# Gates of two chunks from one fp32r product with stacked halves, in a hybrid decoder layer

## The chip, the cores and the metric

The kernel runs on one core of one Trainium2 chip, as one launch. The metric is the device time of that launch in microseconds; the median of three runs is shown, and one further execution was taken with the hardware profiler. The engines are named as in the profile: PE is the matrix engine (PEld its weight loads), DVE the vector engine, ACT the scalar engine, POOL the general engine, SP the engine that issues the DMAs.

## The reference, cut to what matters

One layer of a decoder over 2048 tokens and 16 meta tokens, width 1024, in fp32: an input projection, then side by side a gated linear attention (GLA, 4 heads) and a sliding-window attention, an output projection, and a feed-forward block of width 4096. The change is in the gates of the GLA part:

```
g = log_sigmoid(lr @ w_gate_up + b_gate) / 16     # lr: (tokens, 16), w_gate_up: (16, 256)
b = cumsum(g) within a chunk
o = (A v) + (q * exp(b)) S                        # A from q, k and exp of differences of b
S = exp(b_last) * S + (k * exp(b_last - b))^T v
```

## The kernel before

The dense products (input projection, output projection, feed-forward) split each fp32 operand into a high and a low part of type fp32r and run three fp32r matmuls of 512 columns (lines 160 to 162) for each fp32 one. They are the bulk of PE's work. The two attention parts are Python generators, `gla` and `swa`; the dense code calls `mix_stage` after every 12 matmuls of a product, and each generator then emits its next stage. So the small matmuls of the attention parts stand between the dense ones. The final order of the first half of the program (until about 1100 us) is set by a scheduler that works with its own estimates of durations; engines run their instructions in that order. From there on the order is written out by hand and is not touched.

GLA goes through a chunk of 16 meta tokens and then 16 chunks of 128 tokens, called chunk 0 to chunk 15 here. Each chunk starts with `gates`: a PE transpose of lr (tile `lr`, line 567), a DVE copy into `lrT` (line 568), two plain fp32 matmuls of 128 columns into `z` (line 572; the profile records each as two), three ACT steps and one DVE step of the log-sigmoid into `g` (lines 543 to 546), and two DVE scans into `B` (line 580). `lrT` holds ones below its 16 rows, so that row 16 of the weight `wg` adds the bias. After that come seven levels (`E`, `kl`, `ql` on DVE and ACT, the matmul `lv`, line 677, and the predicated copy `AT`, line 682), `qB` (line 721), the output matmuls `o` and the state update. `sg` is the log-sigmoid of another gate at the end of a chunk, 512 columns wide, with the same four lines 543 to 546.

The projection's weights come in with `raw` and are split by ACT (`wh`, line 125) and DVE (`wl`, line 126). The rotary part of the projection's results is a run of DVE steps (lines 203 to 206) behind the copy `st` (line 243) that empties a PSUM bank.

Of the kernel before, what the change touches and what calls it, by code (L numbers as in the profile page):

```python
# [35 lines left out]
class Layer:  # L36
# [23 lines left out]
    def more_consts(self):  # L60
        nc, a, cp = self.nc, self.a, self.cp
        t = cp.tile([P, 576], F32, name="tabs", tag="tabs")
        nc.sync.dma_start(out=t, in_=a["tabs"])
        self.ident, self.smask = t[:, 0:P], t[:, P:544]
        self.csm = t[:, 544:576].rearrange("p (a n) -> p a n", a=2)
        wide = self.np_.tile([P, len(LEVELS), 64], U32, name="lwide", tag="sq", bufs=3)
        nc.sync.dma_start(out=wide, in_=a["lmask"])
        self.lmask = cp.tile([P, len(LEVELS), 64], U8, name="lmask", tag="lmask")
        nc.vector.tensor_copy(self.lmask, wide)
        self.wg = cp.tile([P, 256], F32, name="wg", tag="wg")  # L70
        nc.sync.dma_start(out=self.wg, in_=a["wg"])
        self.nsink = cp.tile([P, 8], F32, name="nsink", tag="nsink")
        nc.vector.tensor_scalar(self.nsink, self.sinks, -1.0, None, ALU.mult)
# [474 lines left out]
    def gla_setup(self, cp):  # L548
# [6 lines left out]
        for t in self.kl:  # L555
            nc.gpsimd.memset(t, 0.0)
        self.lrT = cp.tile([P, P], F32, name="lrT", tag="lrT")
        nc.vector.memset(self.lrT, 1.0)
# [24 lines left out]
    def decayed_keys(self, gp, B, k, n):  # L583

        nc = self.nc
        kt = gp.tile([P, 2, P], F32, name="kt", tag="g", bufs=1)[:, :, :n]
        nc.vector.tensor_tensor(kt, B[:, :, n - 1 : n].to_broadcast([P, 2, n]), B, ALU.subtract)
# [24 lines left out]
    def gla_load(self, b, gp):  # L612
        nc = self.nc
        qk = gp.tile([P, 4, P], F32, name="qk", tag="qk", bufs=2)
        nc.sync.dma_start(out=qk, in_=self.feat[b // 4, :, F_Q:F_R, (b % 4) * P : (b % 4 + 1) * P])
        v = gp.tile([P, 528], F32, name="v", tag="v", bufs=2)
        nc.sync.dma_start(out=v, in_=self.vals[b, :, 0:528])
        return qk, v

    def gla(self, gp):  # L620
        nc = self.nc
        while self.have_v < 1:
            yield
        ld = self.gla_load(0, gp)
        B = yield from self.gates(gp, self.m_v[:, 512:528], NM)
        kt = self.decayed_keys(gp, B, self.m_k, NM)
# [10 lines left out]
        for b in range(nblk):  # L637
            qk, v = ld
            if b + 1 < nblk:
                while self.have_v <= b + 1:  # L640
                    yield
                ld = self.gla_load(b + 1, gp)
            yield from self.gla_chunk(b, gp, qk, v)
            self.done_g = b + 1
# [41 lines left out]

    def gla_chunk(self, b, gp, qk, v):
# [3 lines left out]
        B = yield from self.gates(gp, v[:, 512:528], P)  # L691
        nc.gpsimd.tensor_copy(self.qpad[0:64, 0], q[0:64])
# [16 lines left out]
        for li in range(len(LEVELS)):  # L709
# [37 lines left out]
        for hp in range(2):  # L747
            for h in range(2):
                rr = slice(64 * h, 64 * h + 64)
                c = hp * 256 + h * P  # L750
                nc.vector.scalar_tensor_tensor(
                    self.S[rr, hp, h, :], self.S[rr, hp, h, :], eB[rr, hp, P - 1 : P], ps[rr, c : c + P],
                    ALU.mult, ALU.add,
                )
# [883 lines left out]
def layout(inp):  # L1638
# [15 lines left out]
    A["w2q"] = f["w_ff2"][0].reshape(16, 2, P, 4, 2, P).transpose(0, 2, 4, 1, 3, 5).reshape(16, P, 2048)  # L1654
    A["wg"] = np.concatenate([f["w_gate_up"][0], f["b_gate"], np.zeros((P - 17, 256), np.float32)], axis=0)
    pos = np.arange(L) + NM
# [37 lines left out]
```

## Time and profile before

| | |
|---|---|
| median of 3 runs (lowest to highest) | 2172.25 us (2171.24 to 2172.98) |
| profiled execution | 2170.22 us, span of the trace 2168.5 us |
| PE busy | 99% of the span |
| DVE, ACT, POOL busy | 71%, 48%, 9% |
| mean granted PE clock | 0.997 |

The span is what the trace covers; the 1.7 us around it belong to the launch. A busy share of PE counts modelled ends of pipelined matmuls: matmuls follow each other closer than their durations, so start times, not durations, tell what one costs.

### The profile page before, as it was taken

Reading aid. Unit: us, or ns where it says so; the run is one execution under the profiler, and the core shown is the slowest. Engines: PE = TensorE matmul, PEld = TensorE weight load, DVE = VectorE, ACT = ScalarE, POOL = GpSimd, SP = SyncE. Lnnn points to the kernel's source line nnn. Section 1 sums busy time; section 2 is a strip of 40 time slices with the busy share of each in tenths; the row PEclk is TensorE's granted clock in tenths of the full one; section 3 lists DMA queues with packets and bytes.
Section 4 is the critical chain, followed back from the end, with each engine's and each line's share of the span. In section 5 each row is a group of like instructions: output and inputs, shape, how many; then the busy total and the mean of one; then the engine's idle time right before and its main releaser. Section 6 shows DMA issues by size and latency. Waiting matters only on the chain.

```text
span 2168.5 us, 29105 instructions
## 1 busy us (share of the span) xinstructions
PE 2141.0 (99%) x10423; PEld 1801.7 (83%) x10423; DVE 1537.9 (71%) x2863; ACT 1046.4 (48%) x2156; POOL 198.8 (9%) x311
## 2 busy tenths in 40 slices
PE   8999999999999999999999999999999999999997
PEld 6998789788888888888888888888888888888886
DVE  7167884988987878789963445456867766685866
ACT  5132754456665656566652323353544545333434
POOL 2000111121221122221110000000000000000001
PEclk9999999999999999999999999999999999999998
DMA  6234533335333333335333335544355557754412
GB/s 212 95 96 134 157 108 111 99 103 188 106 105 104 100 110 105 104 109 168 112 101 99 97 97 155 184 142 141 121 162 178 170 194 264 279 173 138 156 39 78
DMA packets 147857, 292.51 MB, mean 135 GB/s; under 512 B 12288, under 2 KB 64000, under 8 KB 147712
## 3 DMA queue, kind: packets, MB, share of 16 engines
q1 hardware_dynamic: 147712, 290.66, 42.0%
q8 instruction: 82, 1.34, 0.3%
q14 instruction: 63, 0.52, 0.1%
HBM read 220.68 MB, written 69.86 MB: 134 GB/s over the span
## 4 chain that ended last, share of the span: by engine, by line
PE 87%; DVE 7%; ACT 3%; DMA 1%; issue 1%; DVEq 0%; SPq 0%; ACTq 0%
PE psd L162 16%; PE psd L161 16%; PE psd L160 16%; PE psq L160 4%; PE psq L162 4%; PE psq L161 4%; PE psw L160 4%; PE psw L161 4%; PE psw L162 4%; PE lv L677 2%; PE psd L295 2%; PE psd L296 2%; PE psd L297 2%; PE pv L530 1%; DVE wl L126 1%
## 5 line engine op out<-in xcount | busy, mean ns | idle before, releaser
L125 ACT ACTIVATE wh<-raw 128x1024 fp32r<-128x1024 f32 (+2 forms) x190 | 199.1, 1048 | 343.7 <-PE psd L162 297.2
L126 DVE TENSOR_TENSOR wl<-raw,wh 128x1024 fp32r<-128x1024 f32 (+2 forms) x190 | 234.0, 1232 | 74.5 <-ACT wh L125 73.9
L160 PE MATMUL psd<-f,wh 128*128 128x512 f32 x512 | 203.2, 397 | 0.0
L160 PE MATMUL psd<-hid,wh 128*128 128x512 f32 x512 | 202.9, 396 | 0.0
L162 PE MATMUL psd<-f,wh 128*128 128x512 f32 x512 | 200.0, 391 | 0.0
L161 PE MATMUL psd<-f,wl 128*128 128x512 f32 x512 | 199.9, 390 | 0.0
L162 PE MATMUL psd<-hid,wh 128*128 128x512 f32 x512 | 199.7, 390 | 0.0
L161 PE MATMUL psd<-hid,wl 128*128 128x512 f32 x512 | 199.7, 390 | 0.0
L160 PE MATMUL psd<-u,wh 128*128 128x512 f32 x416 | 167.7, 403 | 3.7 <-DVE st L241 2.4
L161 PE MATMUL psd<-u,wl 128*128 128x512 f32 x416 | 163.9, 394 | 3.1 <-DVE wl L126 3.0
L162 PE MATMUL psd<-u,wh 128*128 128x512 f32 x416 | 164.5, 396 | 0.6 <-DVE u L156 0.6
L160 PE MATMUL psw<-bh,wh 128*128 128x512 f32 x392 | 152.5, 389 | 0.0
L161 PE MATMUL psw<-bh,wl 128*128 128x512 f32 x392 | 152.5, 389 | 0.0
L162 PE MATMUL psw<-bl,wh 128*128 128x512 f32 x392 | 152.5, 389 | 0.0
L160 PE MATMUL psq<-oh,wh 128*128 128x512 f32 x384 | 149.8, 390 | 0.0
L162 PE MATMUL psq<-ol,wh 128*128 128x512 f32 x384 | 149.4, 389 | 0.0
L161 PE MATMUL psq<-oh,wl 128*128 128x512 f32 x384 | 149.4, 389 | 0.0
L962 ACT ACTIVATE wh<-rw 128x1024 fp32r<-128x1024 f32 x49 | 52.0, 1061 | 149.7 <-PE psw L162 132.9
L162 PEld LDWEIGHTS psd<-f,wh 128*128 128x128 f32 x512 | 96.1, 188 | 20.8 <-DVE f L156 0.2
L162 PEld LDWEIGHTS psd<-hid,wh 128*128 128x128 f32 x512 | 96.1, 188 | 20.5
L160 PEld LDWEIGHTS psd<-hid,wh 128*128 128x128 f32 x512 | 96.2, 188 | 19.3 <-issue 0.2
L161 PEld LDWEIGHTS psd<-hid,wl 128*128 128x128 f32 x512 | 96.2, 188 | 19.1 <-issue 0.2
(315 smaller groups left out, 5163.3 us busy)
## 6 DMA issues: line engine op xcount, KB each, us to landing
raw<-w SPq DMA_DIRECT2D x132, 512.0 KB, 3.7
b<-hops SPq DMA_DIRECT2D x49, 512.0 KB, 3.5
raw<-wo SPq DMA_DIRECT2D x32, 512.0 KB, 3.8
r<-w SPq DMA_DIRECT2D x32, 512.0 KB, 4.2
rw<-w2q SPq DMA_DIRECT2D x28, 512.0 KB, 6.6
raw<-wf SPq DMA_DIRECT2D x26, 512.0 KB, 4.0
feat<-st SPq DMA_DIRECT2D x52, 256.0 KB, 2.2
hops<-t SPq DMA_DIRECT2D x42, 256.0 KB, 5.0
```

Source lines behind the costliest of these rows:

```text
L125: nc.scalar.activation(wh, raw, AF.Copy)
L126: nc.vector.tensor_tensor(wl, raw, wh.bitcast(F32), ALU.subtract)
L160: nc.tensor.matmul(ps, lhsT=wh, rhs=ah, start=first, stop=False, skip_group_check=skip)
L161: nc.tensor.matmul(ps, lhsT=wl, rhs=ah, start=False, stop=False, skip_group_check=skip)
L162: nc.tensor.matmul(ps, lhsT=wh, rhs=al, start=False, stop=last, skip_group_check=skip)
L295: nc.tensor.matmul(ps, lhsT=ah, rhs=wh, start=kt == 0, stop=False)
L296: nc.tensor.matmul(ps, lhsT=ah, rhs=wl, start=False, stop=False)
L297: nc.tensor.matmul(ps, lhsT=al, rhs=wh, start=False, stop=kt == KT - 1)
L530: nc.tensor.matmul(pv, lhsT=v[:, kv, :], rhs=t, start=i == 0 and t is ph, stop=False)
L677: nc.tensor.matmul(ps[:, hp * P : (hp + 1) * P], lhsT=kl[:, hp, :], rhs=ql[:, :, hp, :], start=True, stop=True)
L962: nc.scalar.activation(wh, src, AF.Copy)
```

## The change

One call of `gates` now serves two chunks (the meta chunk still goes alone). The two transposes of lr go into one PSUM tile of 256 columns. `lrT` becomes an fp32r tile of 256 columns in which rows 0 to 15 and 64 to 79 hold the high part of lr and rows 32 to 47 the low part; the weight `wgr` holds high, high and low parts in the same rows. So one fp32r matmul for each half of the 256 outputs gives all three partial products. The scans of both chunks follow, and the second chunk of a pair starts without gates. lr gets a DMA of its own for each pair; the weight's DMA moves from `more_consts` into `gla`; `g` and `kt` move into the buffers of `sg` and `qB`; the exponential of `B` goes straight into `qB`, and only its last column is kept as `eB`.

```diff
-        self.wg = cp.tile([P, 256], F32, name="wg", tag="wg")
-        nc.sync.dma_start(out=self.wg, in_=a["wg"])
...
-    def gates(self, gp, lr, n):
+    def gates(self, gp, lrs, n):
         nc = self.nc
+        m = len(lrs)
+        w = m * n
         ps = self.gpsum("lr")
-        nc.tensor.transpose(ps[:16, :n], lr, self.ident[:n, :n])
-        nc.vector.tensor_copy(self.lrT[0:16, :n], ps[:16, :n])
+        for j, lr in enumerate(lrs):
+            nc.tensor.transpose(ps[:16, j * n : (j + 1) * n], lr, self.ident[:n, :n])
+        rows = self.lrT.rearrange("p a n -> p (a n)")
+        nc.scalar.activation(rows[0:16, :w], ps[:16, :w], AF.Copy)
+        nc.vector.tensor_tensor(rows[32:48, :w], ps[:16, :w], rows[0:16, :w].bitcast(F32), ALU.subtract)
+        nc.scalar.activation(rows[64:80, :w], ps[:16, :w], AF.Copy)
         yield
         ps = self.gpsum("z")
         for hp in range(2):
             nc.tensor.matmul(
-                ps[:, hp * n : (hp + 1) * n], lhsT=self.wg[:, hp * P : (hp + 1) * P], rhs=self.lrT[:, :n],
+                ps[:, hp * w : (hp + 1) * w], lhsT=self.wgr[:, hp * P : (hp + 1) * P], rhs=rows[:, :w],
                 start=True, stop=True,
             )
-        B = gp.tile([P, 2 * P], F32, name="B", tag="B")[:, : 2 * n]
-        g = gp.tile([P, 2 * P], F32, name="g", tag="g", bufs=1)[:, : 2 * n]
-        self.log_sigmoid(ps[:, : 2 * n], g)
-        for c in (slice(0, n), slice(n, 2 * n)):
-            nc.vector.tensor_tensor_scan(B[:, c], self.ones[:, :n], g[:, c], 0.0, ALU.mult, ALU.add)
-        return B.rearrange("p (a n) -> p a n", a=2)
+        B = gp.tile([P, m, 2, n], F32, name="B", tag="B" if m > 1 else "E", bufs=1 if m > 1 else 2)
+        g = gp.tile([P, NB], F32, name="g", tag="sg", bufs=1)[:, : 2 * w]
+        self.log_sigmoid(ps[:, : 2 * w], g)
+        for j in range(m):
+            for hp in range(2):
+                c = slice(hp * w + j * n, hp * w + (j + 1) * n)
+                nc.vector.tensor_tensor_scan(B[:, j, hp, :], self.ones[:, :n], g[:, c], 0.0, ALU.mult, ALU.add)
+            if j == 0 and m > 1:
+                yield
+        return [B[:, j] for j in range(m)]
...
+        if b % 2 == 0:
+            self.lr = gp.tile([P, 2, 16], F32, name="lr", tag="lr", bufs=2)
+            nc.sync.dma_start(out=self.lr, in_=self.vals[b : b + 2, :, 512:528].rearrange("b p c -> p b c"))
...
+        wg = gp.tile([P, 256], F32, name="wg", tag="qB", bufs=1)
+        wh = gp.tile([P, 256], F32R, name="wgh", tag="kT", bufs=1)
+        nc.sync.dma_start(out=wg, in_=self.a["wg"])
+        nc.scalar.activation(wh, wg, AF.Copy)
+        nc.scalar.activation(self.wgr[0:64], wg[0:64], AF.Copy)
+        nc.vector.tensor_tensor(self.wgr[64:P], wg[64:P], wh[64:P].bitcast(F32), ALU.subtract)
...
+            if b % 2 == 0:
+                Bs = yield from self.gates(gp, [self.lr[:, j, :] for j in range(2)], P)
...
-        eB = gp.tile([P, 2, P], F32, name="eB", tag="eB", bufs=1)
-        nc.scalar.activation(eB, B, AF.Exp, scale=1.0 / 16.0)
+        eB = gp.tile([P, 2, 1], F32, name="eB", tag="eB")
+        nc.scalar.activation(eB, B[:, :, P - 1 : P], AF.Exp, scale=1.0 / 16.0)
         qB = gp.tile([P, 2, P], F32, name="qB", tag="qB", bufs=1)
-        nc.vector.tensor_tensor(qB, q, eB, ALU.mult)
+        nc.scalar.activation(qB, B, AF.Exp, scale=1.0 / 16.0)
+        nc.vector.tensor_tensor(qB, q, qB, ALU.mult)
```

The scheduler makes a new order of the first half from this. Line numbers of the changed kernel differ by 2 above the change and by some 20 below it. Three places follow, each as it was and as it is.

PE at the start of chunk 8, where the product `z` stands between dense matmuls. Before:

```order
L160 MATMUL psd<-hid,wh 128x512
L161 MATMUL psd<-hid,wl 128x512
L162 MATMUL psd<-hid,wh 128x512
L572 MATMUL z<-lrT,wg 128x128 x2
L160 MATMUL psd<-hid,wh 128x512
L161 MATMUL psd<-hid,wl 128x512
```

And with the change:

```order
L158 MATMUL psd<-hid,wh 128x512
L159 MATMUL psd<-hid,wl 128x512
L160 MATMUL psd<-hid,wh 128x512
L578 MATMUL z<-lrT,wgr 128x256 x2
L158 MATMUL psd<-hid,wh 128x512
L159 MATMUL psd<-hid,wl 128x512
```

The place is the same, the two matmuls are twice as wide and of the other type, and at the start of chunk 9 there are none.

DVE late in the second half of the input projection, around the split `wl` of one certain weight (the 33rd one on this engine in both programs) and amid the steps of chunk 3. Before:

```order
L205 TENSOR_TENSOR st<-st,cs 128x512
L503 TENSOR_TENSOR pm_117<-trm,pm_117 64x128
L206 TENSOR_TENSOR st<-st,sw 128x512
L514 TENSOR_TENSOR pl<-tr,ph 128x512
L682 COPY_PREDICATED AT<-lmask,lv 128x256
L721 TENSOR_TENSOR qB<-qk,eB 128x256
L126 TENSOR_TENSOR wl<-raw,wh 128x1024
L695 TENSOR_TENSOR qkp<-qk 128x256
L243 TENSOR_TENSOR st<-psd,rb 128x512
```

And with the change, around the same weight:

```order
L703 COPY_PREDICATED AT<-lmask,lv 128x32x8
L680 TENSOR_TENSOR E<-B 128x256 x2
L414 TENSOR_TENSOR qs<-ft,qs 64x512
L684 TENSOR_TENSOR kl_123<-qk,E 128x64x2
L688 TENSOR_TENSOR ql<-qpad,E 128x256
L124 TENSOR_TENSOR wl<-raw,wh 128x1024
L241 TENSOR_TENSOR st<-psd,rb 128x512
L703 COPY_PREDICATED AT<-lmask,lv 128x64x4
L201 STREAM_SHUFFLE sw<-st 128x512
L684 TENSOR_TENSOR kl_122<-qk,E 128x128
```

Before, the split stood behind all seven levels of chunk 3 and behind `qB`; now it stands behind the fourth level's copy, so three levels and `qB` come after it, and two rotary runs (16 of them stood ahead before, 14 do now).

SP at the start of the program (`x` is the input, `wf` weights of the projection, `cs` rotary tables, `xm` the meta tokens). Before:

```order
L215 DMA x<-x 128x1024
L71 DMA wg<-wg 128x256
L122 DMA raw<-wf 128x1024
L182 DMA xm<-meta 128x128
L215 DMA x<-x 128x1024
L326 DMA cs<-cs 128x1024
```

And with the change:

```order
L213 DMA x<-x 128x1024
L180 DMA xm<-meta 128x128
L120 DMA raw<-wf 128x1024
L324 DMA cs<-cs 128x1024
L213 DMA x<-x 128x1024 x3
```

The gate weight's transfer has left this place (it now stands later, between two of the last transfers of `x`), and the table `cs` has moved ahead of the third transfer of `x`.

## Rows read from the trace of the kernel before

**Rows 1.** The page: busy time of the engines, and the last chain's shares.

```profile
PE 2141.0 (99%) x10423; PEld 1801.7 (83%) x10423; DVE 1537.9 (71%) x2863; ACT 1046.4 (48%) x2156; POOL 198.8 (9%) x311
PE 87%; DVE 7%; ACT 3%; DMA 1%; issue 1%; DVEq 0%; SPq 0%; ACTq 0%
```

**Rows 2.** PE's timeline around the last `z`: start us, us, what.

```profile
1029.38 0.61 PE L572 MATMUL z<-lrT,wg 128*128 128x128 f32 x4
1029.75 0.48 PE L160 MATMUL psd<-m,wh 128*128 128x512 f32 x1
1030.06 0.40 PE L161 MATMUL psd<-m,wl 128*128 128x512 f32 x1
1030.29 0.39 PE L162 MATMUL psd<-m,wh 128*128 128x512 f32 x1
```

**Rows 3.** PE's timeline near the end: fp32r matmuls of 256 columns.

```profile
2149.92 0.28 PE L162 MATMUL psd<-l,h 128*128 128x256 f32 x1
2150.04 0.28 PE L160 MATMUL psd<-h 128*128 128x256 f32 x1
```

**Rows 4.** Tile `z`: durations in ns, min/median/max.

```profile
L543 ACT ACTIVATE g<-z x17: 197/365/386, 113.3 to 1030.2; 128x256 f32<-128x256 f32 x16, 128x32 f32<-128x32 f32 x1
L546 DVE SCALAR_TENSOR_TENSOR g<-z,g x17: 192/424/426, 114.1 to 1031.9; 128x256 f32<-128x256 f32 x16, 128x32 f32<-128x32 f32 x1
```

**Rows 5.** Groups by line and shape: scans, and the 512-column log-sigmoid `sg`.

```profile
L580 DVE TENSOR_TENSOR_SCAN B<-ones,g 128x128 f32<-128x128 f32 x32 | 12.9, 445 | 0.2
L546 DVE SCALAR_TENSOR_TENSOR sg<-r,sg 128x512 f32<-128x512 f32 x16 | 11.3, 709 | 10.4 <-ACT sg L545 10.3
L543 ACT ACTIVATE sg<-r 128x512 f32<-128x512 f32 x16 | 10.1, 629 | 12.8 <-DVE mo L770 11.8 <-DMA r<-feat 0.9
```

**Rows 6.** Tile `lr`: the copy into `lrT`.

```profile
L568 DVE COPY lrT<-lr x17: 163/269/279, 107.4 to 1027.0; 16x128 f32<-16x128 f32 x16, 16x16 f32<-16x16 f32 x1
```

**Rows 7.** The chain that ended last, from 374 to 425 us.

```profile
420.68 1.58 DVE wl L126
422.30 0.50 PE psd L161
```

**Rows 8.** PE's timeline behind that wait (idle before it in brackets).

```profile
422.30 0.50 PE L161 MATMUL psd<-u,wl 128*128 128x512 f32 x1 [1.95 <-DVE wl L126]
423.41 0.63 PE L162 MATMUL psd<-u,wh 128*128 128x512 f32 x1
425.97 0.63 PE L162 MATMUL psd<-u,wh 128*128 128x512 f32 x1
```

**Rows 9.** Windows: busy us (instructions) of each engine, granted clock, DMA.

```profile
core 0: us, PE busy (x) PEld busy (x) DVE busy (x) ACT busy (x) POOL busy (x), PEclk, DMA share, GB/s
410.00:420.00 10.00, 10.00 (x52) 8.11 (x51) 9.79 (x20) 3.71 (x11) 1.14 (x3) 1.00 0.21 68
420.00:430.00 10.00, 8.05 (x37) 6.53 (x36) 8.25 (x14) 1.96 (x11) 1.17 (x2) 0.83 0.70 215
```

**Rows 10.** PE's timeline at the first level of chunk 1.

```profile
269.87 0.68 PE L677 MATMUL lv<-ql,kl 128*128 128x128 f32 x4 [0.72 <-DVE ql L667]
```

**Rows 11.** The chain that ended last, from 240 to 271 us.

```profile
264.94 0.34 DVE g L546
265.87 1.30 DVE B L580 x2
```

**Rows 12.** PE's timeline at the one `z` that waited.

```profile
708.36 0.71 PE L572 MATMUL z<-lrT,wg 128*128 128x128 f32 x4 [0.28 <-DVE lrT L568]
```

**Rows 13.** PE's timeline from 32 us, behind its longest early wait.

```profile
32.07 0.47 PE L160 MATMUL psd<-u,wh 128*128 128x512 f32 x1 [2.21 <-DVE st L241]
32.38 0.39 PE L161 MATMUL psd<-u,wl 128*128 128x512 f32 x1
32.61 0.39 PE L162 MATMUL psd<-u,wh 128*128 128x512 f32 x1
```

**Rows 14.** SP's timeline at the start: DMA issues.

```profile
8.04 0.43 SPq L71 DMA_DIRECT2D wg<-wg  x1
11.51 0.33 SPq L215 DMA_DIRECT2D x<-x  x1
11.88 0.43 SPq L326 DMA_DIRECT2D cs<-cs  x1
```

**Rows 15.** The chain that ended last, at the start: transfers it waits for.

```profile
1.71 4.82 DMA x<-x
11.51 5.34 DMA x<-x
```

More of the change, by code (lines that the diff above doesn't have):

```diff
@@ L556, in gla_setup @@
             nc.gpsimd.memset(t, 0.0)
-        self.lrT = cp.tile([P, P], F32, name="lrT", tag="lrT")
-        nc.vector.memset(self.lrT, 1.0)
+        self.lrT = cp.tile([P, 2, P], F32R, name="lrT", tag="lrT")
+        nc.vector.tensor_scalar(self.lrT, self.ones.unsqueeze(1).to_broadcast([P, 2, P]), 1.0, None, ALU.mult)
+        self.wgr = cp.tile([P, 256], F32R, name="wgr", tag="wgr")
     def gpsum(self, name):
         return self.pm.tile([P, NB], F32, name=name, tag="gl", bufs=2)
-    def gates(self, gp, lr, n):
+    def gates(self, gp, lrs, n):
         nc = self.nc
+        m = len(lrs)
+        w = m * n
         ps = self.gpsum("lr")
-        nc.tensor.transpose(ps[:16, :n], lr, self.ident[:n, :n])
-        nc.vector.tensor_copy(self.lrT[0:16, :n], ps[:16, :n])
+        for j, lr in enumerate(lrs):
[4 more added lines that the diff above has]
+        nc.scalar.activation(rows[64:80, :w], ps[:16, :w], AF.Copy)
         yield
@@ L572, in gates @@
             nc.tensor.matmul(
[L573 removed]
+                ps[:, hp * w : (hp + 1) * w], lhsT=self.wgr[:, hp * P : (hp + 1) * P], rhs=rows[:, :w],
                 start=True, stop=True,
             )
[L576 to L581 removed]
+        B = gp.tile([P, m, 2, n], F32, name="B", tag="B" if m > 1 else "E", bufs=1 if m > 1 else 2)
[8 more added lines that the diff above has]
+        return [B[:, j] for j in range(m)]
     def decayed_keys(self, gp, B, k, n):
         nc = self.nc
[L586 removed]
+        kt = gp.tile([P, 2, P], F32, name="kt", tag="qB", bufs=1)[:, :, :n]
         nc.vector.tensor_tensor(kt, B[:, :, n - 1 : n].to_broadcast([P, 2, n]), B, ALU.subtract)
@@ L613, in gla_load @@
         nc = self.nc
+        if b % 2 == 0:
+            self.lr = gp.tile([P, 2, 16], F32, name="lr", tag="lr", bufs=2)
+            nc.sync.dma_start(out=self.lr, in_=self.vals[b : b + 2, :, 512:528].rearrange("b p c -> p b c"))
         qk = gp.tile([P, 4, P], F32, name="qk", tag="qk", bufs=2)
         nc.sync.dma_start(out=qk, in_=self.feat[b // 4, :, F_Q:F_R, (b % 4) * P : (b % 4 + 1) * P])
-        v = gp.tile([P, 528], F32, name="v", tag="v", bufs=2)
-        nc.sync.dma_start(out=v, in_=self.vals[b, :, 0:528])
+        v = gp.tile([P, NB], F32, name="v", tag="v", bufs=2)
+        nc.sync.dma_start(out=v, in_=self.vals[b, :, 0:NB])
         return qk, v
@@ L621, in gla @@
         nc = self.nc
-        while self.have_v < 1:
+        while self.have_v < 2:
             yield
+        wg = gp.tile([P, 256], F32, name="wg", tag="qB", bufs=1)
[4 more added lines that the diff above has]
+        nc.vector.tensor_tensor(self.wgr[64:P], wg[64:P], wh[64:P].bitcast(F32), ALU.subtract)
         ld = self.gla_load(0, gp)
-        B = yield from self.gates(gp, self.m_v[:, 512:528], NM)
+        (B,) = yield from self.gates(gp, [self.m_v[:, 512:528]], NM)
         kt = self.decayed_keys(gp, B, self.m_k, NM)
@@ L638, in gla @@
             qk, v = ld
+            if b % 2 == 0:
+                Bs = yield from self.gates(gp, [self.lr[:, j, :] for j in range(2)], P)
             if b + 1 < nblk:
-                while self.have_v <= b + 1:
+                while self.have_v <= (b + 1 | 1):
                     yield
                 ld = self.gla_load(b + 1, gp)
-            yield from self.gla_chunk(b, gp, qk, v)
+            yield from self.gla_chunk(b, gp, qk, v, Bs[b % 2])
             self.done_g = b + 1
@@ L685, in gla_level_mm, with gla_chunk @@
         )
-    def gla_chunk(self, b, gp, qk, v):
+    def gla_chunk(self, b, gp, qk, v, B):
         nc = self.nc
@@ L690, in gla_chunk @@
         q, k = qk[:, 0:2, :], qk[:, 2:4, :]
-        B = yield from self.gates(gp, v[:, 512:528], P)
         nc.gpsimd.tensor_copy(self.qpad[0:64, 0], q[0:64])
@@ L751, in gla_chunk @@
                 nc.vector.scalar_tensor_tensor(
-                    self.S[rr, hp, h, :], self.S[rr, hp, h, :], eB[rr, hp, P - 1 : P], ps[rr, c : c + P],
+                    self.S[rr, hp, h, :], self.S[rr, hp, h, :], eB[rr, hp], ps[rr, c : c + P],
                     ALU.mult, ALU.add,
@@ L1654, in layout @@
     A["w2q"] = f["w_ff2"][0].reshape(16, 2, P, 4, 2, P).transpose(0, 2, 4, 1, 3, 5).reshape(16, P, 2048)
-    A["wg"] = np.concatenate([f["w_gate_up"][0], f["b_gate"], np.zeros((P - 17, 256), np.float32)], axis=0)
+    wg = np.zeros((P, 256), np.float32)
+    for r in (0, 32, 64):
+        wg[r : r + 16] = f["w_gate_up"][0]
+    wg[[16, 80]] = f["b_gate"]
+    A["wg"] = wg
     pos = np.arange(L) + NM
```

## The prediction

> **What bounds the kernel now.** I read the page first. PE is busy 99% of the span and 87% of the chain that ended last is PE [rows 1], so a microsecond taken from PE should come off the end. But 7% of the chain is DVE, and that tells of stretches where PE runs behind DVE. Next I read the waits of PE, the chain through the stretches of the first half, and PE's timeline around the product `z`. All edits lie in the first half of the program: after some 1100 us no line of the change runs, and the order there is written by hand. So the sum has two kinds of terms: PE work that goes, and waits of PE that move because a scheduler makes a new order.
>
> The chain from 374 to 425 us shows the second kind. It runs almost without a break on DVE and ends in one split of a weight, 1.58 us, for which PE stood [rows 7]. The windows say the same: DVE is busy 9.79 of 10 us, then PE only 8.05 of 10 [rows 9].
>
> **The change part by part.** The sum is made against the profiled execution, 2170.22 us, which is 2.03 us below the median of the runs shown. The same difference is then taken from the median.
>
> *The product.* Start times tell what `z` costs. Its four records start at 1029.38, the next dense matmul at 1029.75, the one after that at 1030.06 and the third at 1030.29 [rows 2]. From the start of `z` to 1030.06 are 0.68 us. One dense matmul follows another after 0.23 us (1030.06 to 1030.29), so `z` takes 0.45 us from PE: 0.37 of its own and 0.08 because the first dense matmul behind a plain fp32 one holds its successor up by 0.31 instead of 0.23. There are 17 of them (16 chunks and the meta chunk), so 7.65 us.
> The new product is two fp32r matmuls of 256 columns for each pair. The trace has that very shape in the last product: starts 0.12 us apart [rows 3]. That is 0.24 us for a pair and 1.92 for eight. The two matmuls of the meta chunk have 16 columns; I take the same 0.24 as a bound. The type needs no change of pace to the dense matmuls beside it. So 2.2 us in place of 7.65: 5.5 us saved.
> The transposes of lr stay 17 in number and keep their price; they only come in twos. In the order of the changed program a plain fp32 matmul stands directly before an fp32r one at 207 places, before at 226. Of the 19, 15 are the `z` counted already; the other four give 4 x 0.08 = 0.3 us. PE work saved: 5.8 us.
>
> *DVE and ACT.* For a pair, DVE loses two copies of 0.27 [rows 6] and two log-sigmoid steps of 0.42 [rows 4], together 1.39 us. It gains one step of 512 columns, 0.71 [rows 5], and a subtraction of 256 columns out of PSUM, nearest to the 0.42 of [rows 4]. So it is about 0.3 us lighter for a pair. ACT loses six steps of 0.37 to 0.42 and gains three of 0.63 [rows 5], two copies of about 0.37 (by the 256 columns of [rows 4]) and a tiny exponential: some 0.6 us heavier for a pair, hidden because ACT is busy 48% [rows 1]. Neither matters as an amount. What matters is when: the second chunk of a pair gets its gates a whole chunk earlier, so that two scans and a log-sigmoid step, 0.9 + 0.4 us of DVE, and the copy go from the start of every odd chunk and lie in the even one.
>
> *Wait at 420 us.* Here odd chunk 3 shares DVE with the rotary steps. PE stood 1.95 us for the split, and shortly after, six matmuls start 2.56 us apart in all (423.41 to 425.97), 0.43 each instead of 0.23 [rows 8]; the granted clock of that window is 0.83 [rows 9]. So the place costs at least 1.95 + 6 x 0.2 = 3.2 us. In the new order the same split has three levels' steps, `qB` and two rotary runs fewer ahead of it, and chunk 3 has no gates to make: by the durations above far more than 1.95 us of DVE work. The work comes after it instead and could make PE wait later. Bounds: 3.2 us gained, and nothing. I take 2.0, nearer to the full price, since the queue is so much shorter.
> [...] But a wait of 2.21 us at 29.9 us was followed by matmuls at the usual 0.23 (32.38 to 32.61) [rows 13], so a wait of this length does not bring the spell each time.
>
> *First level of chunk 1.* At 269.87 PE stood 0.72 us for `ql` [rows 10]. The chain into it runs over the log-sigmoid and both scans of chunk 1, 1.30 us [rows 11], which will have been made 130 us earlier, beside chunk 0. Bounds: 0.7 us gained; 0.5 lost, should the copies around it fall badly. I take 0.5 gained.
>
> *The step from lr to `z`.* It was one DVE copy; now it is an ACT copy and behind it a DVE subtraction, with a second ACT copy beside them. The extra step costs about 0.4 us and one more turn in a busy queue. It is covered by the 12 dense matmuls (2.7 us) that stand between lr and `z`, in most new places with some attention matmuls more. Before, one of the 17 waited, 0.28 us, and for DVE [rows 12]. If PE waits, everything behind it in its order waits. Bounds: nothing, and 8 x 0.5 = 4 us. I take 1.0 lost.
>
> *The start.* The gate weight's transfer, issued at 8.04, goes from ahead of the third transfer of `x`, and the table `cs` comes in ahead of it [rows 14]. PE's first 25 us run at the pace of `x`: its transfers of 4.82 and 5.34 us are the longest pieces of the chain there [rows 15]. `cs` has 512 KB and the gate weight 128, so that `x` could be late by the difference; I bound it by 0.9 us and zero, as the later transfers have fewer bytes ahead of them than before, and take 0.3 lost. SP issues eight DMAs more, a small one for lr per pair, a whole chunk ahead of its use, so that its queue hides them.
>
> Sum: -5.8 - 2.0 - 0.5 + 1.0 + 0.3 = -7.0 us, that is 2163.2 against the profiled 2170.22, and 2165.3 against the median.
>
> **The rivals.** *The gain goes into DVE.* In the stretches where the chain runs on DVE, shorter PE work only makes PE wait longer: the `z` of chunks 1 to 3 lie there, about 1.1 us of the 5.8. If also the waits at 420 and 270 us only move to another place, and lr to `z` costs 2: -5.8 + 1.1 + 2.0 + 0.3 = -2.4, so 2169.9. For it speaks that DVE loses next to no work; against it, that its busiest stretches hold odd chunks, which get lighter.
>
> *Waits fall away altogether.* If the places at 420 and 270 us give their full price and nothing new waits: -5.8 - 3.2 - 0.7 = -9.7, so 2162.5. For it speaks that every odd chunk gets lighter where DVE is busiest; against it, that a new order of some thousand instructions seldom brings no wait of its own.
>
> *Slower.* The `z` of each pair waits in its longer chain and the clock falls behind it: 8 x (0.5 + 1.2) = 13.6 us lost, against the 8.0 us that the sum gains without this term: +5.6, so 2177.8. It decides from 1.0 us lost per pair. Against it: one wait of 0.28 in 17, with cover left in the others.
>
> *The product is no faster.* If fp32r at 256 columns cost what fp32 does, the 5.5 us are lost: -1.5, so 2170.8. [rows 3] speak plainly against it.
>
> **How the numbers follow.** Forecast 0.51, gain into DVE 0.28, waits fall away 0.13, slower 0.06, no faster product 0.02. A measurement of this kernel can tell about 0.2%, 4.3 us, from no change, so faster means below 2167.9. The forecast's own range is 2162.5 to 2168.5; nine tenths of it, all of the third case and a fifth of the second lie below 2167.9: 0.46 + 0.13 + 0.06 = 0.65. Slower is 0.06, the same 0.29. The range for all, 2161.0 to 2170.5, goes some 1.5 us below the third case, for odd chunks that I did not cost, and leaves out the slower case, a third of the second and most of the last.
>
> **What would show it.** Right: `z` as 18 records of type fp32r with starts 0.12 us apart and the next dense matmul 0.12 behind, no 0.31 after it; PE's wait for `wl` at about 420 us gone or under 0.5 us, and the clock at 1.00 in that window; no idle time before the first level of chunk 1; PE waiting for `lrT` in at most two of eight places. Wrong: several waits for `lrT` with a lower clock behind them; a wait for `st`, `kl` or `ql` of over 1 us between 415 and 435 us; PE's dense work in the first 25 us shifted by a microsecond; or `z` starting over 0.2 us apart.

## The result, and the profile after

The changed kernel takes 2159.83 us, the median of four runs (2156.96 to 2160.91); the kernel before takes 2171.74 us beside it. The ratio is 0.9943 (95% interval 0.9931 to 0.9956): about 12 us faster, where 7 were forecast. The time lies 1.2 us below the low end of the range given.

The profiled execution lies near the upper end of the four: 2160.74 us, with a span of 2159.0 us. The page of the changed kernel, in the two lines that answer to [rows 1]:

```profile
PE 2135.2 (99%) x10373; PEld 1798.4 (83%) x10373; DVE 1533.2 (71%) x2848; ACT 1056.4 (49%) x2168; POOL 202.1 (9%) x311
PE 89%; DVE 6%; ACT 3%; DMA 2%; issue 1%; SPq 0%; DVEq 0%; ACTq 0%
```

PE has 50 matmul records fewer, and DVE's share of the chain fell from 7 to 6%. The product `z`, on PE's timeline (start us, us, what), which answers to [rows 2]:

```profile
645.96 0.39 PE L160 MATMUL psd<-hid,wh 128*128 128x512 f32 x1
646.18 0.40 PE L578 MATMUL z<-lrT,wgr 128*128 128x256 f32 x2
646.42 0.40 PE L158 MATMUL psd<-hid,wh 128*128 128x512 f32 x1
646.65 0.40 PE L159 MATMUL psd<-hid,wl 128*128 128x512 f32 x1
```

From the start of `z` to the start of the second matmul behind it are 0.47 us; less one usual step of 0.23 that is 0.24 for two chunks, where one chunk took 0.45. The next view is the windows around 420 us, which answer to [rows 9] (us, busy us and instructions of PE, PEld, DVE, ACT and POOL, granted clock, DMA):

```profile
410.00:420.00 10.00, 10.00 (x51) 8.42 (x50) 9.42 (x19) 3.07 (x9) 1.19 (x2) 1.00 0.43 137
420.00:430.00 10.00, 10.00 (x56) 8.57 (x56) 9.25 (x21) 3.09 (x13) 2.00 (x2) 1.00 0.42 131
```

PE does not stand at all, the granted clock is 1.00, and DVE is nearly as full as it was. All that the view of PE's waits lists between 105 and 1150 us (us in total, times, longest):

```profile
PE sc L467 <- DVE qs L413: 0.7, 1, 0.7
PE oT L789 <- DVE o L762: 0.5, 1, 0.5
PE psn L97 <- DVE acc L92: 0.3, 1, 0.3
PE sc L467 <- DVE sst L469: 0.2, 1, 0.2
```

These are 1.7 us. The same view of the kernel before adds up to 5.0 us; its first five entries are:

```profile
PE psd L161 <- DVE wl L126: 2.0, 1, 2.0
PE lv L677 <- DVE ql L667: 0.7, 1, 0.7
PE sc L469 <- DVE sst L471: 0.6, 2, 0.4
PE lr L567 <- PE pv L531: 0.4, 1, 0.4
PE psd L295 <- ACT st L302: 0.4, 1, 0.4
```

Of the wait for `wl` and of the first level `lv` nothing is left. New is a spell of the lower clock that the kernel before did not have at this place, on PE's timeline at 275 us:

```profile
275.65 1.12 PE L97 MATMUL psn<-acc,ones 128*128 128x512 f32 x2 [0.33 <-DVE acc L92]
276.62 1.84 PE L113 MATMUL psn<-ones,acc 128*128 128x1 f32 x16
278.64 0.51 PE L160 MATMUL psd<-u,wh 128*128 128x512 f32 x1
278.95 0.63 PE L158 MATMUL psd<-u,wh 128*128 128x512 f32 x1
279.38 0.63 PE L159 MATMUL psd<-u,wl 128*128 128x512 f32 x1
```

Seven dense matmuls from 278.95 on start 0.43 us apart, at a granted clock of 0.50 (278.9 to 282.0 us), which costs 7 x 0.2 = 1.4 us.

For the comparisons below I use a stretch that holds the whole change and leaves out the noisy start: from the first `lr` of the meta chunk to the first `psq`, in the part whose order is fixed by hand. Before it runs from 107.22 to 1530.16 us, 1422.94; after from 109.05 to 1521.36, 1412.31. That is 10.6 us shorter, with the 1.4 us of the spell in it. The time ahead of the stretch is 1.8 us longer in this one execution.

### The profile page after: what moved, and what is told of

Same layout as the page of the kernel before. It is cut to its first block, busy times and chain, and to the rows that moved or that the text cites. A ratio compares the mean times of both kernels' runs of the same rounds, so it can differ in the third digit from the quotient of the medians.

```text
span 2159.0 us, 29009 instructions
## 1 busy us (share of the span) xinstructions
PE 2135.2 (99%) x10373; PEld 1798.4 (83%) x10373; DVE 1533.2 (71%) x2848; ACT 1056.4 (49%) x2168; POOL 202.1 (9%) x311
## 4 chain that ended last, share of the span: by engine, by line
PE 89%; DVE 6%; ACT 3%; DMA 2%; issue 1%; SPq 0%; DVEq 0%; ACTq 0%
PE psd L158 16%; PE psd L160 16%; PE psd L159 16%; PE psq L158 4%; PE psq L160 4%; PE psq L159 4%; PE psw L158 4%; PE psw L160 4%; PE psw L159 4%; PE lv L698 2%; PE psd L293 2%; PE psd L294 2%; PE psd L295 2%; PE pv L528 1%; PE kv L616 1%
```

## The experiments

Each kernel ran beside the kernel before on the same chip. The stretch and PE's waits (the sum of the view shown above, 105 to 1150 us) come from each kernel's one profiled execution.

| kernel | median us | ratio to before (95%) | stretch us | PE's waits us |
|---|---|---|---|---|
| before | 2170.15 to 2171.74 | | 1422.9 | 5.0 |
| changed | 2159.83 | 0.9943 (0.9931 to 0.9956) | 1412.3 | 1.7 |
| pair_fp32 | 2165.20 | 0.9974 (0.9965 to 0.9983) | 1416.6 | 2.5 |
| single_fp32r | 2169.05 | 0.9990 (0.9981 to 0.9999) | 1420.5 | 6.3 |
| wg_early | 2159.78 | 0.9946 (0.9933 to 0.9958) | 1411.7 | 1.2 |
| before_wg_late | 2171.51 | 1.0006 (0.9997 to 1.0015) | 1423.0 | 4.5 |
| before_eB | 2171.05 | 0.9993 (0.9984 to 1.0003) | 1423.6 | 4.9 |
| before_lr_dma | 2169.68 | 0.9997 (0.9988 to 1.0006) | 1420.8 | 4.6 |
| before_wl_pool | 2170.07 | 0.9995 (0.9986 to 1.0004) | 1422.4 | 5.4 |
| double_z | 2161.09 | 0.9953 (0.9941 to 0.9966) | 1412.7 | 1.5 |
| late_scans | 2159.91 | 0.9947 (0.9935 to 0.9960) | 1410.7 | 1.4 |
| late_logsig | 2163.18 | 0.9963 (0.9951 to 0.9976) | 1413.1 | 3.3 |
| late_stage | 2165.22 | 0.9977 (0.9968 to 0.9986) | 1415.5 | 2.8 |
| early_stage | 2169.03 | 0.9992 (0.9983 to 1.0001) | 1419.4 | 7.2 |
| copies_first | 2158.70 | 0.9939 (0.9926 to 0.9953) | 1409.7 | 1.5 |

**The type alone taken back (pair_fp32).**

```diff
-        self.lrT = cp.tile([P, 2, P], F32R, name="lrT", tag="lrT")
+        self.lrT = cp.tile([P, 2, P], F32, name="lrT", tag="lrT")
...
-        self.wgr = cp.tile([P, 256], F32R, name="wgr", tag="wgr")
+        self.wgr = cp.tile([P, 256], F32, name="wgr", tag="wgr")
...
-        nc.vector.tensor_tensor(rows[32:48, :w], ps[:16, :w], rows[0:16, :w].bitcast(F32), ALU.subtract)
-        nc.scalar.activation(rows[64:80, :w], ps[:16, :w], AF.Copy)
...
```

> Pairing kept, the product back to plain fp32 (unsplit weight, one copy of lr, no subtraction). Theory A, the gain has two halves of about equal size, PE work (about 5 us, nearly all of it the product) and waits of the first half that the early gates of odd chunks take away (about 5 us): the product costs about 0.9 us a pair again, the work comes back and the waits stay away, so about 5 us slower than the changed kernel, 2165, and no wait of PE over 1 us at about 420 us. Theory B, the product and the type switches carry nearly all of the gain: about 2170. Theory C, the waits carry nearly all of it: about 2161.

It took 2165.2, the time of theory A. PE's timeline shows the product of this kernel:

```profile
646.58 1.02 PE L576 MATMUL z<-lrT,wgr 128*128 128x256 f32 x4
647.25 0.58 PE L158 MATMUL psd<-hid,wh 128*128 128x512 f32 x1
647.67 0.40 PE L159 MATMUL psd<-hid,wl 128*128 128x512 f32 x1
```

From 646.58 to 647.67 are 1.09 us, less 0.23: 0.86 for a pair in plain fp32, against 0.24. Eight times the difference is 5.0 us, and the medians differ by 5.4. So fp32r is worth 5 us here, nearly all that the prediction had for the product. The rest, 6 us, comes with the pairing even in plain fp32, and there the waits are 2.5 us instead of 5.0. This kernel also has one copy in place of three steps between lr and `z`, so it lacks the small delays of `z` that copies_first takes up below.

**The pairing alone taken back (single_fp32r).**

```diff
             if b % 2 == 0:
-                Bs = yield from self.gates(gp, [self.lr[:, j, :] for j in range(2)], P)
+                lrs = self.lr
+            (B,) = yield from self.gates(gp, [lrs[:, b % 2, :]], P)
...
```

> The stacked fp32r product kept, but made for each chunk alone at its own start (128 columns, 17 chains from lr to z instead of 9, no gates ahead of time). Theory A: the work of PE stays low (two matmuls of at most 0.12 us a chunk, so about 4.1 us for all instead of 2.4: 1.7 us of the 5 lost), and the waits come back, the one at about 420 us and the one before the first level of chunk 1 with them: about 4 to 5 us, so 2165 to 2167. Theory B (product alone): 2160 to 2162, whatever the waits. Theory C (waits alone): 2167 to 2170.

It took 2169.05, above theory A's bracket and within theory C's. The product is cheap: from 649.76 to 650.22 are 0.46, less 0.23 is 0.23 a chunk, 3.9 us for 17. But the waits have come back, and more of them than before. First PE's timeline at the product, then the three largest of its waits:

```profile
649.76 0.33 PE L578 MATMUL z<-lrT,wgr 128*128 128x128 f32 x2
649.93 0.45 PE L158 MATMUL psd<-hid,wh 128*128 128x512 f32 x1
650.22 0.39 PE L159 MATMUL psd<-hid,wl 128*128 128x512 f32 x1
```

```profile
PE z L578 <- ACT lrT L574: 1.7, 1, 1.7
PE psd L159 <- DVE wl L124: 1.6, 1, 1.6
PE lr L570 <- issue: 1.4, 1, 1.4
```

The wait for `wl` at 417 us stands, 1.6 us instead of 1.95, `lr` waits 1.4 us at 431, and one `z` waits 1.7 us for its input, with a spell of the lower clock behind it (the dense matmuls at 706.94 and 707.32 us start 0.38 us apart). The cheaper product alone saves 3.7 us (7.65 less 3.9), of which 2 are left in the medians. So neither half of the change would have been worth 12 us by itself: alone they give 2 and 6 us by the medians, and the last 4 come only with both.

**The order of transfers at the start (wg_early, before_wg_late).** One puts the gate weight's transfer of the changed kernel back into `more_consts`, the other moves that of the kernel before into `gla`, with nothing else.

```diff
+        self.wg = self.gp.tile([P, NB], F32, name="wg", tag="B", bufs=1)[:, :256]
+        nc.sync.dma_start(out=self.wg, in_=a["wg"])
...
```

> The changed kernel with the gate weight's transfer back at its old place at the start, so that SP issues the first 24 transfers in the order of before. Theory A: the order of transfers costs the changed kernel about 1.5 us in the first 60 us (meta's lr stood 1.8 us later than before by the two profiles): 1 to 2 us faster than the changed kernel, 2158 to 2159, and lr of the meta chunk comes at about 107 us in the trace again. Rival: those 1.8 us were spells of the lower clock that come and go between executions, so no difference of the medians, 2160, and the same spread.

> The kernel before with only the gate weight's transfer moved, so that SP's order at the start is that of the changed kernel. Theory A: 1 to 2 us slower than before, 2173, and the wait of about 2 us for wl at about 420 us stays, since odd chunks still make their gates at their own start. Rival: the wait at 420 us is an accident of the scheduler's order and any edit moves it: it is gone or under 0.5 us, and the time is 2168 to 2170. Second rival: the start's order costs nothing: 2172, and the wait stays.

The medians are 2159.78 and 2171.51: no difference from the kernels that they come from. In wg_early `lr` of the meta chunk still stands at 109.1 us; over all profiled kernels it lies between 107.0 and 109.1 with the weight's transfer at its old place and between 107.4 and 110.9 at its new one. Most of that spread goes with the clock. In three executions the granted clock of the first 50 us is 1.00, and `lr` stands at 107.0 and 107.2 (before_wl_pool and before, old place) and at 107.4 (single_fp32r, new place); in all others it is 0.90 to 0.97, and `lr` stands at 108.1 or later at either place. So the new place costs some 0.2 to 0.4 us by these three, with one execution at the new place, and the medians show 0 and 0.4. In before_wg_late the stretch is 1423.0 us, the same as before, and the wait at 420 us is there (1.9 us). So the wait is not an accident that any edit removes, and such a stretch repeats closely where the order is the same.

**The side edits (before_eB, before_lr_dma).** The kernel before with the new `qB` alone, and that with lr's own transfer for each pair besides.

```diff
-        eB = gp.tile([P, 2, P], F32, name="eB", tag="eB", bufs=1)
-        nc.scalar.activation(eB, B, AF.Exp, scale=1.0 / 16.0)
+        eB = gp.tile([P, 2, 1], F32, name="eB", tag="eB")
+        nc.scalar.activation(eB, B[:, :, P - 1 : P], AF.Exp, scale=1.0 / 16.0)
...
```

> The kernel before with the side edit alone: the exponential of B goes straight into qB and a tiny one keeps the last column. Theory A: nothing of the gain comes from it, 2171 to 2172, and the waits stand where they stood. Rival: the scheduler's order changes with it and the waits at 270 and 420 us go or grow: 2168 to 2174.

> The kernel before with lr in a tile and a transfer of its own for each pair and the loads of a pair waiting for both chunks' values, as in the changed kernel (and the side edit of qB, which was worth nothing and makes the room); gates still one chunk at a time in plain fp32. If the loads carry part of the gain: 2167 to 2169, and the wait of lr at 435 us goes. If not: 2171 to 2172, with the waits where they were.

Neither differs from before by the medians, and both keep the wait at 420 us (1.9 us). The new buffers of `g` and `kt` were not tried by themselves. One row of before_lr_dma matters all the same, its window from 420 to 430 us:

```profile
420.00:430.00 10.00, 7.89 (x42) 6.43 (x42) 9.39 (x18) 2.95 (x13) 1.41 (x2) 1.00 0.64 201
```

PE stood 1.91 us as before, but the granted clock is 1.00 where [rows 9] have 0.83. That makes 1.2 of the 2.2 us by which its stretch is shorter than before. In before_wg_late and before_eB, with waits of 1.92 and 1.90 us at this place, dense matmuls behind it start 0.43 us apart as in the kernel before. So the spell that the prediction priced at 1.2 us came behind a wait of this length here in three of four executions, and not in the fourth.

**The wait at 420 us by itself (before_wl_pool).** The kernel before with the one split of a weight on POOL. PE's order is unchanged.

```diff
...
-        nc.vector.tensor_tensor(wl, raw, wh.bitcast(F32), ALU.subtract)
+        (nc.gpsimd if pool else nc.vector).tensor_tensor(wl, raw, wh.bitcast(F32), ALU.subtract)
...
-            return self.split_w(a["wf"][f].rearrange("p k c -> p (k c)"))
+            return self.split_w(a["wf"][f].rearrange("p k c -> p (k c)"), pool=hf == 1 and f == 3)
```

> The kernel before with one split of a weight, the one that PE waited for at 420 us, moved from DVE to POOL; PE's order is the same as before, row for row. Theory A, the place costs its full price (1.95 us of waiting and six matmuls of 0.2 us extra at the lower clock): about 3.2 us faster than before, 2168, with the stretch from lr of the meta chunk to 1091 us shorter by 3 us. Rival, the wait only moves: PE runs into the next DVE result (the copy st or the next split) and at most 1 us is gained, 2170 to 2171.

The wait and the spell are gone (mean granted clock 0.998, in the kernel before 0.997), and the stretch is only about 0.6 us shorter, with a ratio that cannot be told from 1. The time went into other waits, on PE's timeline:

```profile
399.12 0.50 PE L530 MATMUL pv<-pl,vc 128*128 128x512 f32 x1 [0.61 <-DVE pl L514]
406.47 0.68 PE L677 MATMUL lv<-ql,kl 128*128 128x128 f32 x4 [0.83 <-DVE ql L667]
435.55 0.27 PE L567 MATMUL lr<-tabs,v 128*16 128x128 f32 x1 [1.51 <-issue]
```

The wait of `lr` grew from 0.43 to 1.51 us; it starts just behind two DVE steps of the state update (they end at 435.45 us), which read `kv`, a tile of the two PSUM buffers that `lr` uses as well. The first two lie ahead of 420 us, and they have another cause. The timelines show POOL's split, the step that DVE made beside it, and the same step in the kernel before:

```profile
394.44 2.89 POOL L126 TENSOR_TENSOR wl<-raw,wh 128x1024 fp32r<-128x1024 f32 x1 [3.83 <-ACT wh L125]
```

```profile
394.98 2.37 DVE L475 SCALAR_TENSOR_TENSOR sst<-sst,nsink 128x4 f32<-128x4 f32 x1
```

```profile
395.51 0.15 DVE L475 SCALAR_TENSOR_TENSOR sst<-sst,nsink 128x4 f32<-128x4 f32 x1
```

A DVE step of four columns ends with POOL's split, at 397.3 us, and takes 2.37 us instead of 0.15. So DVE was spared the 1.58 us of the split at 420 us but lost 2.2 us at 395, and its queue did not get lighter. What the wait at 420 us is worth by itself this run cannot show, and it stays open; that its time is handed on to the next wait is not shown either.

**The product's price in place (double_z).** The changed kernel with each `z` run twice (`for hp in (0, 1, 0, 1)`).

> The changed kernel with each z product run twice (the second run writes the same values again). Theory A, the product is on the path that sets the end and costs what its starts say, 0.115 us a matmul: 18 more of them give 2.1 us, 2162. Rival, part of it lies beside waits: under 1 us, 2160 to 2161. Second rival, it costs more than its starts say (it holds up the dense matmul behind it, as plain fp32 did): over 3 us, 2163 or more.

It took 2161.09, 1.3 us more, and the intervals overlap. The profile is clearer: a pair's block takes twice as long (0.48 us from 645.36 to 645.84 instead of 0.24) with nothing added behind it, so 18 more matmuls cost about 2.1 us. The stretch grew by 0.4 us only, but the spell of 1.4 us at 279 us was not in this execution. That agrees with 0.115 us a matmul on the path; the medians alone cannot tell the three expectations apart.

**What of the early gates counts (late_scans, late_logsig).** In both, PE's work is that of the changed kernel. In the first the second chunk's scans wait for its own start; in the second its log-sigmoid does too.

```diff
...
+        if b % 2 == 1:
+            self.scans(B, P)
```

```diff
...
+        if b % 2 == 1:
+            self.gate_sums(gp, B, B, P)
```

`scans` is the two scans of a chunk, `gate_sums` has three ACT steps and one DVE step ahead of them. Both kernels split the 512-column steps of a pair that they move into two of 256, and late_logsig has one more ACT copy a pair, so some ACT and DVE work comes in with them.

> The changed kernel, but the scans of the second chunk of a pair (0.9 us of DVE) are left until that chunk's own start, and the log-sigmoid's last step is two of 256 columns instead of one of 512; PE's work is that of the changed kernel. Theory A, the waits went away because DVE is free of the gates where odd chunks begin: part of them comes back, 1 to 3 us slower than the changed kernel, 2161 to 2163, with waits at 270 to 275 and 415 to 435 us. Rival, they went away because the chain from lr over z to B is gone from the odd chunks (an exchange between PE, ACT and DVE, not an amount of work): the scans alone bring nothing back, 2160.

> The changed kernel, but only lr, lrT and z stay early for the second chunk of a pair: its half of z is copied out of PSUM, and the whole log-sigmoid (three ACT steps, one DVE step) and both scans are made at that chunk's own start, as before. Theory D (after late_scans: the waits went because the odd chunks no longer begin with an exchange between PE and the full DVE queue, lr to lrT to z): nothing comes back, 2160, and no wait over 1 us between 380 and 450 us. Theory E (they went because the log-sigmoid's chain is gone from the odd chunk): the waits at 270 and 420 to 435 us come back, 2163 to 2166.

The scans bring nothing back: 2159.91. With the log-sigmoid some comes back: 2163.18, and PE's waits are 3.3 us, led by this one:

```profile
429.97 0.63 PE L795 MATMUL oT<-tabs,o 128*128 128x128 f32 x4 [1.20 <-DVE o L768]
```

The time is at the low end of theory E's bracket, and theory D, with 2160 and no wait over 1 us here, does not hold; of the two places that E named, only the one at 430 us came back. With the steps of single_fp32r, where lr and `z` are late as well, it is a series: 1.4, 3.3 and 6.3 us of waits as more of the gates goes back to the odd chunk's start, where before had 5.0.

**The place in the order (late_stage, early_stage).** The changed kernel with an empty stage more at the start of odd chunks, and with one stage fewer for a pair. PE's matmuls are the same 10373 in all three.

```diff
+        if b % 2 == 1:
+            yield
```

```diff
-            if j == 0 and m > 1:
-                yield
```

> The changed kernel with one empty stage at the start of each odd chunk, so that its levels and results come one stage of 12 dense matmuls later, about as before. Theory F, the odd chunk's place against the projection's steps is what took the waits away (with fewer stages it falls elsewhere in DVE's order): the waits at about 420 to 435 us come back at least in part, 2162 to 2165. Theories D and E: nothing comes back, 2160.

> The changed kernel with one stage fewer for each pair (the scans of both chunks are made in the stage of the product), so that the attention parts run one stage of 12 dense matmuls shorter a pair; it is the opposite of late_stage, whose added waits (1 us of idle time and as much around it) lay at 980 to 1046 us, where the attention parts run out of dense work beside them, and not at 420 us. If the length of the attention parts matters: the waits at 1024 to 1068 us (0.5 us for oT among them) go, 0.5 to 2 us faster than the changed kernel, 2158 to 2159. If the changed kernel already has all that its order can give: 2160, and a wait or two somewhere else. If DVE gets too much at once in even chunks (four scans behind each other): new waits of 1 us or more at 265 to 280 and 380 to 440 us, 2162 or more.

They took 2165.22 and 2169.03. Late_stage has no single large wait; those that the changed kernel does not have lie at 397 (0.4 us), 453 (0.2) and 980 to 1030 us (1.4). So theory F, the place at 420 us, is not borne out, but neither are D and E, which had 2160; and these waits make up 2.0 of the 4.6 us by which the stretch is longer once the spell at 279 us, absent here, is taken off the changed kernel. Early_stage loses nearly all of the gain. Its time is that of the third expectation, but its largest waits lie elsewhere, at 950 and 1005 us. The timelines around the one at 950 us, of DVE, of ACT and of PE in this order:

```profile
949.41 1.22 DVE L124 TENSOR_TENSOR wl<-raw,wh 128x1024 fp32r<-128x1024 f32 x1
950.54 1.12 DVE L865 TENSOR_TENSOR hid<-fr,hid 128x512 fp32r<-128x512 f32 x1
951.69 0.41 DVE L573 TENSOR_TENSOR lrT<-lr,lrT 16x256 fp32r<-16x256 f32 x1
```

```profile
949.41 0.36 ACT L572 ACTIVATE lrT<-lr 16x256 fp32r<-16x256 f32 x1
952.14 0.37 ACT L574 ACTIVATE lrT<-lr 16x256 fp32r<-16x256 f32 x1 [1.85 <-DVE lrT L573]
```

```profile
952.56 0.50 PE L578 MATMUL z<-lrT,wgr 128*128 128x256 f32 x2 [1.83 <-ACT lrT L574]
953.98 0.63 PE L159 MATMUL psd<-f,wl 128*128 128x512 f32 x1
954.40 0.63 PE L160 MATMUL psd<-f,wh 128*128 128x512 f32 x1
```

This is the prediction's slower rival in one place: the subtraction stands behind a split and another DVE step, `z` waits 1.83 us, and a spell of the lower clock follows (dense matmuls 0.42 us apart, 953.98 to 954.40). In these rows a step that has its input still stands behind the step ahead of it on its engine: the subtraction needs only the ACT copy that ended at 949.77 us, and starts at 951.69, when the step ahead of it is done (951.66).

**The chain from lr to z (copies_first).** The rows above also show the second ACT copy behind the subtraction. This kernel has it ahead.

```diff
-        nc.vector.tensor_tensor(rows[32:48, :w], ps[:16, :w], rows[0:16, :w].bitcast(F32), ALU.subtract)
         nc.scalar.activation(rows[64:80, :w], ps[:16, :w], AF.Copy)
+        nc.vector.tensor_tensor(rows[32:48, :w], ps[:16, :w], rows[0:16, :w].bitcast(F32), ALU.subtract)
```

> The changed kernel with the second ACT copy into lrT issued ahead of DVE's subtraction instead of behind it. In the traces that copy starts only after the subtraction (1.20 us later at 964.87 us in the changed kernel, and PE's waits for z of 1.7 and 1.8 us in single_fp32r and early_stage end with it), so the chain from lr to z has three steps in a row, where two were forecast with a copy beside them. If that third step is what made z start late at four of the eight pairs (0.1 to 0.2 us each): those delays go, the stretch from lr of the meta chunk to the first psq gets 0.3 to 0.6 us shorter, no difference of the medians that can be told, 2159 to 2160. If DVE's queue alone makes them: no difference in the stretch either.

In the changed kernel `z` is late at four of eight pairs; one of them on its timeline, and below it the same pair in copies_first:

```profile
857.72 0.39 PE L160 MATMUL psd<-hid,wh 128*128 128x512 f32 x1
858.08 0.50 PE L578 MATMUL z<-lrT,wgr 128*128 128x256 f32 x2
858.42 0.39 PE L158 MATMUL psd<-hid,wh 128*128 128x512 f32 x1
```

```profile
856.02 0.39 PE L160 MATMUL psd<-hid,wh 128*128 128x512 f32 x1
856.25 0.40 PE L578 MATMUL z<-lrT,wgr 128*128 128x256 f32 x2
856.48 0.40 PE L158 MATMUL psd<-hid,wh 128*128 128x512 f32 x1
```

From the matmul ahead of `z` to the one behind it are 0.70 us in the first and 0.46 in the second. Over the four pairs the delays are 0.4, 0.1, 0.2 and 0.2, together 0.9 us where 0.3 to 0.6 were expected, and none of them is left. The stretch is 2.6 us shorter, of which 1.4 are the spell at 279 us, absent here, and about 0.9 these delays. The median of 2158.70 is the lowest of all kernels; its difference to the changed kernel is within what the medians can tell.

## Why the prediction was right in direction and short in size

*The product: right.* Forecast 5.5 us saved; 17 x 0.45 became 8 x 0.24 and 0.14 for the meta chunk, so 5.6. pair_fp32 confirms that it lies on the path. The 18 records, the 0.12 us between starts and the missing 0.31 behind them are as foretold.

*lr to z: right in size, wrong in the picture.* Forecast 1.0 us lost, measured 0.9. It was put as an extra step "with a second ACT copy beside them"; the copy ran behind the subtraction instead, so the chain has three steps. `z` was late in four places, not "at most two of eight", though by little. That the size came out is luck in part: the 1.0 was taken between bounds of 0 and 4 us.

*The start: small, as forecast.* Forecast 0.3 lost. The profiled execution lost 1.8, most of which goes with the lower clock of its first 50 us (0.93); three executions at a granted clock of 1.00 give 0.2 to 0.4, and the two kernels with that edit alone turned round show 0 and 0.4 by the medians.

*The waits: the step that failed.* The wait at 420 us was put at -2.0 and the first level of chunk 1 at -0.5, and every other wait of PE but that of `z` at nothing. Both went in full: the idle times were 1.95 and 0.72 us. With them went waits that the sum did not have: that of `lr` at 436 us (0.43), of `sc` at 389 (0.39) and of a dense matmul for `st` at 326 (0.39). New ones are small (`oT` 0.50, `psn` 0.33, and that of `sc` at 205 us grew from 0.36 to 0.72). Without the `z` of [rows 12] the view of waits went from 4.7 to 1.7 us, 3.0 less. The place at 420 us took 2.11 us over the usual step for 1.95 of idle time; if the others cost 0.16 us beyond their idle time as well, four waits fewer are another 0.6. The spell at 423 us is 1.2. That makes -4.8 where the sum had -2.5. The rival that the waits fall away altogether (2162.5, given 0.13) comes nearest, but the time lies 2.7 us below that one too, and 1.7 us of waits are left.

The fault in the sum was to let a third of the two places' price come back (2.5 taken of 3.9) and to put the smaller waits at nothing without a reason; its range names them only as "odd chunks that I did not cost". From 374 us on, the chain of the kernel before runs mostly on DVE for 50 us; in the changed kernel the 20 us from 405 to 425 are PE's alone, though DVE is 9.3 of 10 us busy there. DVE is no less loaded, but PE's next operand is not the one at the end of its queue. The pairing is needed for this, as the waits show, 2.5 us with it alone (pair_fp32) and 6.3 without it (single_fp32r); it is not enough, as early_stage has the pairs too and 7.2 us of waits. Which part of the pairing counts is shown only in part: the scans at the odd chunk's start cost nothing (late_scans), the log-sigmoid there brings a wait of 1.20 us at 430 us (late_logsig), and with the whole exchange of lr, `z`, log-sigmoid and scans back, the waits for `wl` and of `lr` stand again (single_fp32r).

*The clock.* The sum had the spell at 420 us as part of the place's price. Of the five kernels with that wait, three have it (in before and before_wg_late the granted clock from 400 to 450 us is 0.97); before_lr_dma (1.91 us idle, 1.00 from 420 to 430) and single_fp32r (1.56, 1.00 from 400 to 450) do not. The slower case priced a spell behind the wait of each of eight `z`, and no run shows that: in the changed kernel `z` was late at four pairs, and the 512-column matmuls behind three of them start 0.22 to 0.24 us apart (from 539.58, 858.42 and 965.63 us); early_stage and single_fp32r each have one `z` whose wait, 1.83 and 1.72 us, had a spell behind it. The changed kernel's profile has a spell at 279 us, and so has wg_early (granted clock 0.97 from 250 to 300 us in both), but copies_first, late_scans and double_z do not have it. So the spells are worth 1.2 to 1.4 us an execution either way, and explain part of why the profiled execution was slower than the median.

*What adds up, and what does not.* In the profiled stretch: -5.6 for the product, +0.9 for its delays less the 0.3 of [rows 12], -3.0 for the other idle times, some -0.6 for what goes with four waits fewer, -1.2 and +1.4 for the spells: -8.4 of the 10.6. Some 2 us lie in steps of 0.1 to 0.3 us, the 0.3 forecast for the fewer changes of type among them, and were not assigned one by one; what made them stays open. Without the spell at 279 us the stretch would be 12.0 us shorter, without either spell 10.8; the medians show 11.9.

*What stays open* is why exactly this order suits DVE. Three others with the same matmuls cost 3, 5 and 9 us more (late_logsig, late_stage, early_stage). That the time depends on the placing of the stages is shown; a rule by which the better placing could be told ahead is not. The early gates alone do not make all of the gain, since two of the three have them in full.

## What to carry to other kernels

Where the chain runs on one engine over tens of microseconds, price that stretch with all its waits, the small ones too: here moving an exchange out of the odd chunks took 4.8 us of waits and what goes with them, where 2.5 were forecast for the two largest. Ask of a batched step what it does to the chunk that no longer has it; here that was worth as much as the cheaper product. When an experiment moves a step to another engine, look at what the first engine does meanwhile: here DVE lost more beside POOL's split (2.2 us) than it was spared (1.58). And write parts of one tile that different engines fill in the order in which they are ready, the longest queue last; that took away 0.9 us of delays in one profiled execution, too little for the medians to tell.

## What the runs showed of the hardware

A pair of fp32r matmuls cost the same at 128 columns (0.23 us, single_fp32r) as at 256 (0.24, the changed kernel), so the second chunk's columns were free. Doubled to 256 columns, the pair in plain fp32 took 0.86 us (pair_fp32) against 0.45 at 128 (before).

The length of a wait did not tell whether the lower clock (0.50 granted from 423.4 to 426.0 us of the kernel before) follows. Idle times of 1.95 us (before), 1.92 (before_wg_late), 1.90 (before_eB), 1.83 (early_stage) and 1.72 (single_fp32r) were followed by dense matmuls 0.38 to 0.43 us apart, one of 1.91 us (before_lr_dma) was not, and neither was this one of early_stage, the longest of these, whose next dense matmuls start 0.23 us apart:

```profile
1005.72 0.39 PE L467 MATMUL sc<-kr,qs 128*128 128x272 f32 x1 [2.52 <-DVE sst L469]
1006.08 0.39 PE L158 MATMUL psd<-hid,wh 128*128 128x512 f32 x1
1006.31 0.39 PE L159 MATMUL psd<-hid,wl 128*128 128x512 f32 x1
```

In the changed kernel a spell came behind only 0.33 us of idle time and sixteen matmuls of one column; in pair_fp32 the same group behind 0.36 us was followed by matmuls 0.23 us apart. Five of the waits here were followed by a spell and two about as long or longer were not, so by these runs a spell cannot be added to a wait's price as certain.

A split of 1024 columns took 2.89 us on POOL, against a mean of 1.24 us on DVE, and a DVE step of four columns beside it took 2.37 us instead of 0.15 (before_wl_pool).
